# Side work in two places of each block, gates one at a time, and PE in order of emission

## The chip, the core and the metric

The kernel runs on one core of a Trainium2 chip. Time is device time in microseconds (us) of one execution. The engines are PE (TensorE, matrix products), DVE (VectorE), ACT (ScalarE), POOL (GpSimd) and SP (SyncE, which here issues most of the DMA transfers). Each has its own queue and works through it in order. The program is built once: a scheduler fixes the order of every queue when the program is built, and semaphores make the engines wait for one another when it runs.

## The reference

One block of a diffusion backbone: a modulated RMS norm of 4096 tokens of 1024 features, one input projection whose 3072 columns feed two groups, and one output projection.

```python
pl = (rms_norm(xl, norm_g[l]) * (1.0 + sc_l) + sh_l) @ w_in[l]
hf_c, hb_c = rglru_bidir(pc[..., r0:r1], *rnn_p, zero, zero)            # 256 context tokens
hf_l, hb_l = rglru_bidir(pl[..., r0:r1], *rnn_p, hf_c[:, -1], hb_c[:, 0])
# rglru: r = sigmoid(xc @ wa + ba); i = sigmoid(xc @ wx + bx); a = exp(-8 r softplus(-lam))
#        b = sqrt(1 - a^2) * i * xc; h_t = a_t h_(t-1) + b_t, forward and backward
u = dwconv(p[..., :3 * D_HYENA], hy_conv_w, (1, 1)) + hy_conv_b
x0, x1, v = jnp.split(u, 3, axis=-1)
y_h = long_conv(v * x1, kernel, hy_bias) * x0                           # FFT of length 2 x 4096
y = concat([rms_norm(y_h, gn_h) * silu(z_h), rms_norm(hf + hb, gn_r) * silu(z_r)])
xl = xl + g_l * (y @ w_out)
return rms_norm(xl, final_g)
```

The kernel of the long convolution is itself computed: a small network over positions with sines (`mlp`), a product to 1024 filter columns, a decay.

## The kernel before

**Tiling.** Every product is made of three 16-bit products (high by high, high by low, low by high). A block of the input projection (`inproj`, L501) is one strip of 128 output features for 512 tokens: 8 slices of 128 input features times 3 products, 24 matmuls of 512 columns into one bank of tag `mm`, of which there are three. These are the main matmuls. 512 tokens are a chunk. All other matmuls are side work (`mms`, L170, a lower priority for the scheduler) and use tags `fa` and `fb`, two banks each, or `sm`, one bank.

**Pass A** (`pass_a`, L579) goes through chunks 0 to 7, with 12 blocks each: 4 of the recurrent input `xr` and 8 of `x1` and `v`. The list `OX` says how many of the other blocks come before the `xr` blocks in each chunk. A block is followed by its short convolution on ACT and DVE (`conv`) and by stores. The next chunk is loaded, normed, split and transposed beside it (`xload`, `xsplit`).

**Pass B** (`blocks_b`, L1024) has 24 groups of 4 blocks (`zr`, `x0`, `zh`), over chunks from 7 down to 0 in the order of `seq`. Beside it runs a generator `fft` from which `rate` steps are pulled per block: first the transform of the input (`s1u_gen`, evictions `vo`), then 64 slots (`slot_gen`: loads `vu`, `vki`, `tb`, 24 matmuls of 128 columns, a product, a transpose, 3 matmuls of the inverse, eviction `zo` and a store), then the inverse (`inv_block`). The output phase (`phase_out`) multiplies by the output weights.

**Side work and steps.** A counter `step` rises by one per block. `at(d, f)` (L561) files a piece of side work for `d` steps later; `tick` (L565), called after each block, runs what is filed for the step. So all side work of a block is emitted behind its 24 main matmuls. The scheduler then orders each engine's queue, PE's too, by its own estimate of when operands are ready, and may put main matmuls of later blocks ahead of side work that waits.

- `unit` (L804) is a generator for the recurrent part of two strips of features: a split of the input (`xh`), the gates, tanh and exponentials, square roots, scans. Gates: for each lane `l` and gate `g`, 3 matmuls into `fa` (g = 0) or `fb` (g = 1) and a sigmoid on ACT (L824). Two units (`p` = 0, 1) advance together. All gates of a unit lie in one step, 24 matmuls for the two units. `DA` files the steps of pass A (`units_a`, L855), `DC` those of the context, `DS` and `D0` those of pass B (`units_b`, L1092), which end in a total over features (`yscale`, L1147) and a store.
- `filter_group` (L952) files four rows of the filter. `filter_row` (L967) first runs the second half of an earlier row (`second`, `fb`), then 3 matmuls into `fa`, a product with the decay `dec`, a split `kh` and a sum on POOL.
- `wprep` (L463) makes scaled weights: a sum of squares, a total over partitions by a matmul (`total`, L186, operand `p2b`), a scale, a split, and 24 matmuls of 2 columns against `shl` for the bias. `wpair` (L621) runs all of that for two strips in each of the first four steps of chunk 0; `prep` spreads it over three steps in chunk 7.

Of the kernel before, what the change touches and what calls it, by code (L numbers as in the profile page):

```python
# [25 lines left out]
FFT = 1.75  # L26
INV = 1.65
LAG = 3
DC = (1, 2, 4, 5, 5)
CT = 5  # L30
ML = 1
MK = 1
# [10 lines left out]
FL = (2, 3)  # L43
SIDE = 64
FG = 2
OX = (0, 0, 0, 0, 0, 0, 2, 0)
ET = mybir.EngineType
MS = ()
XS = ((1, 2), (1, 2))
PB = {"mm": 3, "fa": 2, "fb": 2, "sm": 1}  # L50
FD = 4.95
XK = ((6, 9), (1, 6))
NX = 11
D0 = (8, 11, 12, 13, 14, 16, 17, 17)
WO = (9, 13, 16)
SEQ = [(2, "zr"), (2, "x0"), (1, "x0"), (1, "zr"), (0, "x0"), (0, "zh"), (0, "zr"), (2, "zh"), (1, "zh")]
XL = [(6, "zr"), (5, "zr"), (4, "zr"), (3, "zr"), (2, "zr"), (1, "x0"), (0, "x0"), (2, "zh")]
DS = (1, 4, 7, 7, 9, 9, 10)
DA = ((11, 12, 14, 15, 15), (3, 4, 4, 6, 6), (0, 3, 5, 6, 8))
EPS = 1e-6  # L60
MAGIC = 1.5 * 2.0 ** 23
INV2PI = 1.0 / (2.0 * math.pi)
# [100 lines left out]
class K:  # L163
# [32 lines left out]
    def build(self):  # L196
        tc = self.tc
        with ExitStack() as es:
            self.dram = es.enter_context(tc.tile_pool(name="dram", bufs=1, space=DRAM))
            self.cp = es.enter_context(tc.tile_pool(name="cp", bufs=1))  # L200
            self.ps = es.enter_context(tc.tile_pool(name="ps", bufs=1, space=PSUM))
            dr = lambda n, s, d=F32: self.dram.tile(s, d, name=n)
            self.s1D = dr("s1D", [2, D])
            self.gD = dr("gD", [1, D])
            self.XD = [dr(f"XD{i}", [128, 2, 8, 512], F16) for i in range(6)]
            self.uD = [dr(f"uD{b}", [128, T]) for b in range(NB)]
            self.VuD = dr("VuD", [128, NB, 64, 256], F16)
            self.VkD = dr("VkD", [128, 64, 1024], F16)
            self.ZD = dr("ZD", [128, 64, 1024], F16)
            self.hD = dr("hD", [128, 2, 64, 64], F16)  # L210
            self.xcD = [dr(f"xcD{b}", [128, T]) for b in range(NB)]
            self.hfD = [dr(f"hfD{b}", [128, T]) for b in range(NB)]
            self.x0D = [dr(f"x0D{b}", [128, T]) for b in range(NB)]
            self.zD = [dr(f"zD0{b}", [128, T]) for b in range(NB)]
            self.hlD = dr("hlD", [128, 8, 2, NB, 512], F16)
            self.consts()
            self.wp = es.enter_context(tc.tile_pool(name="wp", bufs=1))
            self.xp_ = es.enter_context(tc.tile_pool(name="xq", bufs=1))
            self.late = es.enter_context(ExitStack())
            self.todo = {}  # L220
            self.step = 0
            if MS:
                es.enter_context(tc.manual_schedule(engines=set(MS)))
            self.pass_a()
            self.pass_b()
            self.phase_out()
# [271 lines left out]
            w[5] = self.tap_scales(pool, name, j, es[:, 0:1], be[:, 0:1])  # L498
        yield w

    def inproj(self, w, xs):  # L501
        ps = self.pst("mm", 3)
        c = 0
        for x in xs:
            n = x.shape[-1]
            i = 0
            for k in range(8):
                for (wi, xi) in ((0, 0), (0, 1), (1, 0)):
                    self.mm(ps[:, c:c + n], w[0][:, wi, k, :], x[:, xi, k, :], i == 0, i == 23)
                    i += 1  # L510
            c += n
        return ps
# [48 lines left out]
    def at(self, d, f):  # L561

        self.todo.setdefault(self.step + d, []).append(f)

    def tick(self):  # L565
        for f in self.todo.pop(self.step, []):
            f()
        self.step += 1
# [10 lines left out]
    def pass_a(self):  # L579
        tc, nc, a = self.tc, self.nc, self.a  # L580
        with ExitStack() as es, ExitStack() as right:
# [3 lines left out]
            W = {}  # L585
            self.wn = -1
            X = self.xtile()
# [70 lines left out]
            halo = {nm: None for nm in names}  # L658
            nb = [(n, j) for n in ("x0", "zr", "zh") for j in range(NB)]
            self.WB, self.X = {}, {}  # L660
            for i in range(8):
                xcs = []
                for k, nm in enumerate(names[4:4 + OX[i]] + names[:4] + names[4 + OX[i]:]):
                    if i < 7 and k in XK[i > 0]:
# [5 lines left out]
                        if h and i < 5:  # L670
                            self.at(XS[i > 0][1] + 1, lambda i=i, X=Xn: nc.sync.dma_start(self.XD[i + 1], X))
                    j = nm[1]
                    ps = self.inproj(W[nm], [X])
                    p0 = 512 * i - 1 + (1 if i == 0 else 0)
                    if nm[0] == "xr":
                        if j % 2 == 0:
# [29 lines left out]
                X = Xn  # L706
            while any(s < self.step + 8 for s in self.todo):
                self.tick()
    def ctx_in(self, ap, hy, W):
# [18 lines left out]
        for j in range(NB):  # L728
# [3 lines left out]
            if j % 2 == 0:  # L732
# [5 lines left out]
                   for p in range(2)])  # L738
        for d in DC:
            self.at(d, lambda: next(us))  # L740
# [62 lines left out]

    def unit(self, pool, lanes, n, xc, fin, sig=None):  # L804

        nc = self.nc
        L = len(lanes)
        x2 = xc[:, :2 * n]
# [7 lines left out]
        for l, (d, j) in enumerate(lanes):  # L816
            for g, dst, bias in ((0, R, 68 + 4 * d + j), (1, I, 76 + 4 * d + j)):
                for q0 in range(0, n, 512):
                    m = min(512, n - q0)
                    c = n * (j % 2) + q0  # L820
                    ps = self.pst("fa" if g == 0 else "fb", 2)
                    for k, (gi, xi) in enumerate(((0, 0), (0, 1), (1, 0))):
                        self.mms(ps[:, :m], self.gh[d][:, gi, j, g, :], xh[:, 1026 * xi + c:1026 * xi + c + m], k == 0, k == 2)
                    nc.scalar.activation(dst[:, n * l + q0:n * l + q0 + m], ps[:, :m], AF.Sigmoid,  # L824
                                         bias=self.ccol(bias), scale=self.rg[d])
        if sig:
            sig()
        for l in range(0, L, 2):
# [16 lines left out]
        for l, (d, j) in enumerate(lanes):  # L845
            f = (lambda t: t) if d == 0 else (lambda t: t[:, ::-1])
# [105 lines left out]
    def filter_group(self, pool, g):  # L952

        nc = self.nc
        grp = [4 * g + 4 + k for k in range(4)] if g < 15 else [1, 2, 3, 0]
        hb = self.hb[g % 2]
        n0 = min(grp)
        for h in range(2):
            nc.sync.dma_start(hb[64 * h:64 * h + 64, :, :, 64 * h:64 * h + 64],
                              self.hD[64 * h:64 * h + 64, :, n0:n0 + 4, :])  # L960
        dec = pool.tile([128, 4, 512], F32, name="dec", bufs=1)
        for k, n in enumerate(grp):
            nc.scalar.activation(dec[:, k], self.dl, AF.Exp, scale=self.dcol[:, n:n + 1])
        for k, n in enumerate(grp):
            self.at(1 + k, lambda k=k, n=n: self.filter_row(pool, n, hb[:, :, n - n0, :], dec[:, k]))

    def filter_row(self, pool, n, hb, dec):  # L967
        nc = self.nc
        if len(self.sec) > 1:
            self.sec.pop(0)()  # L970
        ps = self.pst("fa", 2)
        for x, (hi, wi) in enumerate(((0, 0), (0, 1), (1, 0))):
            self.mms(ps, hb[:, hi, :], self.whl[:, wi, :], x == 0, x == 2)
# [50 lines left out]
    def blocks_b(self, hy, rn):  # L1024
        tc, nc = self.tc, self.nc
        fft = self.fft_gen()
        gate = self.gate_gen()
        W = self.WB
# [3 lines left out]
        st, X = {}, self.X  # L1032
        done, rate = 0.0, FFT
        for q, (i, nm) in enumerate(seq):
            if (i, nm) in XL:
                k = need.pop(0)
# [12 lines left out]
                    self.at(d, lambda g=st[i]: next(g))  # L1049
            for j in range(NB):  # L1050
                w = W[nm, j]
                ps = self.inproj(w, [X[i]])
                if nm == "zr":
                    if j % 2 == 0:
                        z = rn.tile([128, 1024], F32, name="zr", bufs=2)
# [10 lines left out]
                    if i in (5, 4):  # L1066
                        self.pull(gate, 1)
                self.tick()
                done += rate
                while done >= 1:  # L1070
                    done -= 1
                    self.pull(fft, 1)
                if (i, nm, j) == (0, "x0", 3):
                    self.pull(fft)
                    fft = self.inv_gen()
                    done, rate = 0.0, INV
# [15 lines left out]
    def units_b(self, rn, i):  # L1092
# [14 lines left out]
        def sig(p):  # L1107
            def f():
# [4 lines left out]
        us = zip(*[self.unit(rn, [(1, 2 * p), (1, 2 * p + 1)], 512, xcs[p],  # L1113
                             lambda h, p=p: self.padd(hfs[p], hfs[p], h[:, :1024]), sig(p) if i else None)
                   for p in range(2)])
        for _ in range(4):
            next(us)
            yield
        next(us)
# [431 lines left out]
```

## Time and profile before

| | |
|---|---|
| time, median of 3 runs | 2286.21 us (2283.73 to 2293.96) |
| profiled execution, own time | 2286.44 us |
| its span, first to last instruction | 2284.6 us |
| mean granted clock of PE | 0.927 of full speed |
| busy: PE, DVE, ACT, POOL | 1920.0, 1498.6, 1151.6, 862.5 us |
| matmuls | 10858 |

An engine's idle time is put down to what ended it: "PE fa <- ACT R" is PE waiting to write a bank of tag `fa` or for an operand, until ACT's instruction that writes `R` was done. PE's busy time is the union of its matmuls' lengths, so that matmuls at the lower clock count longer.

### The profile page before, as it was taken

The page shows a single profiled execution, that of the slowest core. Times are in us where ns is not written, and L with a number is a line of the kernel's source. Part 1 is how long each engine was busy: PE and PEld are TensorE (multiplying, and loading weights), DVE is VectorE, ACT ScalarE, POOL GpSimd, SP SyncE. Part 2 cuts the span into 40 slices and gives each one's busy share as a digit, 9 for nine tenths or more (in the row PEclk, how much of TensorE's full clock was granted, in tenths as well). Part 3 has the DMA queues.
Part 4 walks back from the last instruction along what each step waited for, and adds up shares of the span by engine and source line. Part 5 has one row for each costly group of instructions (what it writes and reads, how often), then busy time and mean ns, then how long its engine had stood idle before and what let it go on. Part 6 is the DMA issues. An engine that isn't in the chain of part 4 may idle for free. (4 is left out here: it accounts for less than half of the span.)

```text
span 2284.6 us, 30912 instructions
## 1 busy us (share of the span) xinstructions
PE 1920.0 (84%) x10858; PEld 919.7 (40%) x10858; DVE 1498.6 (66%) x2871; ACT 1151.6 (50%) x1803; POOL 862.5 (38%) x571
## 2 busy tenths in 40 slices
PE   6967769989797889878888999797897766999987
PEld 2434324334343334433334555454544433444433
DVE  4895876857576677664644664755756645777776
ACT  3655766665646577575563633645444412422222
POOL 3024655554656453131322443534433321333330
PEclk9988979989898999999899999998998887999999
DMA  9546244435453322566646999899997799454531
GB/s 291 172 115 168 77 137 137 154 81 162 138 150 96 112 87 96 179 196 207 208 143 210 205 217 249 200 227 244 221 257 206 189 270 230 136 163 155 168 120 74
DMA packets 397608, 391.13 MB, mean 171 GB/s; under 512 B 209513, under 2 KB 295935, under 8 KB 392846
## 3 DMA queue, kind: packets, MB, share of 16 engines
q1 hardware_dynamic: 376988, 342.25, 54.2%
q10 hardware_dynamic: 20466, 46.93, 7.2%
q8 instruction: 85, 1.39, 0.3%
q14 instruction: 69, 0.57, 0.1%
HBM read 213.96 MB, written 132.13 MB: 151 GB/s over the span
## 5 line engine op out<-in xcount | busy, mean ns | idle before, releaser
L168 PE MATMUL mm<-X,wh 128*128 128x512 f16 x3072 | 745.8, 389 | 35.4 <-DMA X<-xh 7.5
L168 PEld LDWEIGHTS <-wh 128*128 128x128 f16 x3648 | 326.5, 100 | 466.9 <-issue 102.3
L168 PE MATMUL mm<-X,wz 128*128 128x512 f16 x1536 | 384.8, 395 | 7.5 <-ACT zh L1064 4.5
L168 PEld LDWEIGHTS <-wz 128*128 128x128 f16 x1728 | 159.9, 101 | 226.7 <-issue 58.0
L168 PEld LDWEIGHTS <-hl 128*128 128x128 f16 x1536 | 151.8, 101 | 212.2 <-issue 20.8
L168 PE MATMUL mm<-wz,hl 128*128 128x512 f16 x768 | 181.8, 395 | 18.9 <-DVE hl L1465 13.4
L168 PE MATMUL mm<-X,hl 128*128 128x512 f16 x768 | 179.9, 389 | 7.7 <-DVE wh L1479 5.3
L985 POOL TENSOR_TENSOR kh<-kd,kh 128x512 f16<-128x512 f32 x64 | 84.5, 1321 | 157.4 <-ACT kh L984 157.4
L460 POOL TENSOR_TENSOR I<-I,xc 128x1024 f32<-128x1024 f32 (+3 forms) x36 | 84.1, 2340 | 128.8 <-ACT I L824 114.8
L1241 POOL TENSOR_TENSOR A<-A,B 128x256 f32<-128x256 f32 x64 | 51.0, 797 | 205.9 <-DVE B L1240 187.8
L452 POOL TENSOR_TENSOR xlo<-xt,xh 128x1024 f16<-128x1024 f32 x32 | 76.8, 2414 | 135.8 <-ACT xh L450 135.8
L168 PE MATMUL fb<-tb,vki 128*128 128x128 f16 x768 | 98.1, 225 | 20.6 <-DMA tb<-in_t_s 19.7
L168 PE MATMUL fa<-xh,gh 128*128 128x512 f16 (+3 forms) x228 | 67.4, 396 | 52.2 <-ACT R L824 42.8
L460 POOL TENSOR_TENSOR zr<-zr,sg 128x1024 f32<-128x1024 f32 x16 | 39.1, 2443 | 176.1 <-ACT sg L1110 176.1
L460 POOL TENSOR_TENSOR xh<-R 128x1024 f32<-128x1024 f32 (+2 forms) x34 | 69.4, 2044 | 79.2 <-ACT R L835 77.7
L1252 DVE SCALAR_TENSOR_TENSOR yy<-A,yy 128x512 f16<-128x512 f32 x64 | 57.7, 902 | 62.1 <-ACT yy L1251 62.0
L841 DVE SCALAR_TENSOR_TENSOR xc<-xh,xc 128x1024 f32<-128x1024 f32 (+2 forms) x34 | 58.2, 1714 | 60.7 <-POOL xh L460 60.3
L168 PE MATMUL fa<-tb,vu 128*128 128x128 f16 x768 | 97.0, 225 | 0.0
L457 POOL TENSOR_TENSOR acc<-acc,dec 128x512 f32<-128x512 f32 x64 | 93.7, 1464 | 4.9 <-ACT dec L978 4.9
L849 DVE TENSOR_TENSOR_SCAN I<-R,car,I 128x512 f32<-128x512 f32 (+2 forms) x64 | 94.6, 1502 | 0.1
L168 PEld LDWEIGHTS <-gh 128*128 128x128 f16 x456 | 46.7, 105 | 111.6 <-issue 70.5
L168 PEld LDWEIGHTS <-vki 128*128 128x128 f16 x768 | 76.7, 100 | 33.7 <-issue 24.5
(377 smaller groups left out, 3723.4 us busy)
## 6 DMA issues: line engine op xcount, KB each, us to landing
VkD<-vk SPq DMA_DIRECT2D x64, 256.0 KB, 2.0
VuD<-vo SPq DMA_DIRECT2D x64, 256.0 KB, 2.5
X<-XD SPq DMA_DIRECT2D x8, 2048.0 KB
vu<-VuD SPq DMA_DIRECT2D x128, 128.0 KB, 3.3
vki<-VkD SPq DMA_DIRECT2D x128, 128.0 KB, 3.6
ZD<-zo SPq DMA_DIRECT2D x64, 256.0 KB, 4.3
xt<-in_x SPq DMA_DIRECT2D x30, 512.0 KB, 5.1
XD<-X SPq DMA_DIRECT2D x6, 2048.0 KB
```

Source lines behind the costliest of these rows:

```text
L168: self.nc.tensor.matmul(out, lhsT, rhs, start=start, stop=stop)
L452: nc.gpsimd.tensor_sub(xl, xt, xh)
L457: self.nc.gpsimd.tensor_add(out, x, y)
L460: self.nc.gpsimd.tensor_mul(out, x, y)
L841: nc.vector.scalar_tensor_tensor(Z, M, 1.0, Z, op0=OP.add, op1=OP.mult)
L849: nc.vector.tensor_tensor_scan(f(h), f(r), f(h), 0.0 if c is None else c, op0=OP.mult, op1=OP.add)
L985: nc.gpsimd.tensor_sub(kh[:, 1], kd, kh[:, 0])
L1241: nc.gpsimd.tensor_sub(A[:, :, 0, :], A[:, :, 0, :], B[:, :, 1, :])
L1252: nc.vector.scalar_tensor_tensor(yy[:, :, 1, :], yv, 0.125, yy[:, :, 0, :], op0=OP.mult, op1=OP.subtract)
```

## The change

- `inproj` takes a function `mid`, called between the fourth and the fifth of its 8 slices. What is filed for a half step is run there, so side work has two places per block: between the halves of the 24 main matmuls and behind them. In pass B half of `rate` is pulled from `fft` at each of the two places.
- `unit` yields after each gate, so that the gates of one lane and kind (6 matmuls for the two units) are a step of their own. `DC`, `DA`, `DS` and `D0` get more entries, with half steps.
- The second half of a filter row is filed for the half step ahead of the next row.
- In chunk 1, four `x1` and `v` blocks come before the `xr` blocks.
- From the first chunk on, to the end of the program, PE takes its instructions in the order of emission. The other engines' queues are still ordered by the scheduler.

```diff
-DC = (1, 2, 4, 5, 5)
+DC = (1, 2, 2, 2.5, 2.5, 3, 3, 3.5, 3.5, 4, 5, 5)
...
-OX = (0, 0, 0, 0, 0, 0, 2, 0)
+OX = (0, 4, 0, 0, 0, 0, 2, 0)
...
-D0 = (8, 11, 12, 13, 14, 16, 17, 17)
+D0 = (8, 11, 11.5, 12, 12.5, 13, 13, 14, 16, 17, 17)
...
-DS = (1, 4, 7, 7, 9, 9, 10)
-DA = ((11, 12, 14, 15, 15), (3, 4, 4, 6, 6), (0, 3, 5, 6, 8))
+DS = (1, 3, 3.5, 4.5, 5.5, 7, 7, 9, 9, 10)
+DA = ((11, 12, 12.5, 13, 13.5, 14, 15, 15), (1, 2, 2.5, 3, 3.5, 4, 5, 6), (0, 2, 2.5, 3.5, 4.5, 6, 7, 9))
...
+                if mid and k == 4:
+                    mid()
                 for (wi, xi) in ((0, 0), (0, 1), (1, 0)):
                     self.mm(ps[:, c:c + n], w[0][:, wi, k, :], x[:, xi, k, :], i == 0, i == 23)
...
+    def mid(self):
+        for f in self.todo.pop(self.step - 0.5, []):
+            f()
+
     def tick(self):
+        self.mid()
         for f in self.todo.pop(self.step, []):
             f()
         self.step += 1
...
+            self.es.enter_context(tc.manual_schedule(engines={ET.PE}))
             for i in range(8):
...
-                    ps = self.inproj(W[nm], [X])
+                    ps = self.inproj(W[nm], [X], self.mid)
...
+                if (l, g) != (L - 1, 1):
+                    yield
         if sig:
             sig()
...
         for k, n in enumerate(grp):
+            self.at(0.5 + k, lambda: len(self.sec) > 1 and self.sec.pop(0)())
             self.at(1 + k, lambda k=k, n=n: self.filter_row(pool, n, hb[:, :, n - n0, :], dec[:, k]))
...
-        if len(self.sec) > 1:
-            self.sec.pop(0)()
...
+                def mid():
+                    nonlocal done
+                    self.mid()
+                    done += rate / 2
+                    while done >= 1:
+                        done -= 1
+                        self.pull(fft, 1)
+                ps = self.inproj(w, [X[i]], mid)
...
-                done += rate
+                done += rate / 2
...
-        for _ in range(4):
+        for _ in range(7):
             next(us)
             yield
```

## Rows read from the trace of the kernel before

**Rows 1.** The profile's page: span, and busy time by engine (share of span, instructions).
```profile
span 2284.6 us, 30912 instructions
...
PE 1920.0 (84%) x10858; PEld 919.7 (40%) x10858; DVE 1498.6 (66%) x2871; ACT 1151.6 (50%) x1803; POOL 862.5 (38%) x571
```
**Rows 2.** Stretches: length; busy PE, PEld, DVE, ACT, POOL (count); clock, DMA share, GB/s.
```profile
61.00:206.00 145.00, 110.03 (x853) 60.39 (x851) 121.03 (x363) 83.18 (x143) 32.17 (x20) 0.89 0.52 145
206.00:917.00 711.00, 604.83 (x2803) 264.24 (x2804) 494.09 (x865) 459.07 (x771) 376.18 (x235) 0.92 0.41 121
...
206.00:335.00 129.00, 93.33 (x395) 39.46 (x396) 92.72 (x149) 89.96 (x143) 71.10 (x41) 0.87 0.34 102
335.00:421.00 86.00, 79.05 (x357) 35.13 (x357) 55.84 (x98) 56.41 (x94) 48.31 (x32) 0.98 0.48 140
...
1258.00:1700.00 442.00, 389.91 (x2873) 220.96 (x2873) 276.98 (x438) 213.41 (x345) 178.46 (x162) 0.97 0.95 226
```
**Rows 3.** PE timeline (start, length of the run); then PE's groups in 206 to 917.
```profile
336.67 12.54 PE L168 MATMUL mm<-X,wh 128*128 128x512 f16 x54
...
L168 PE MATMUL sm<-shl,wh 128*128 128x2 f16 x168 | 6.2, 164 | 1.0 <-ACT wh L478 0.7 <-DVE wh L483 0.2
```
**Rows 4.** What PE waited for in 206 to 917: us in total, times, longest.
```profile
PE fa L168 <- ACT R L824: 32.7, 6, 14.5
PE fb L168 <- DVE car L851: 14.0, 1, 14.0
...
PE fb L168 <- DVE vk L996: 11.0, 2, 10.4
```
**Rows 5.** The same for 61 to 206, 917 to 1258 and 1258 to 1700.
```profile
PE fa L168 <- ACT R L824: 7.2, 2, 6.3
...
PE fa L168 <- DVE vo L1201: 32.3, 13, 8.9
...
PE fb L168 <- DMA tb<-in_t_s: 19.7, 13, 3.4
PE fb L168 <- DVE zo L1266: 7.6, 5, 5.2
```
**Rows 6.** Timelines of POOL, ACT and PE around 690: start, length, [idle before <- releaser].
```profile
682.62 1.26 POOL L457 TENSOR_TENSOR xt<-xt,rp 128x512 f32<-128x512 f32 x1 [5.08 <-issue]
...
687.46 2.56 ACT L963 ACTIVATE dec<-dl,dcol 128x512 f32<-128x512 f32 x4 [8.54 <-POOL acc L457]
...
694.90 1.44 PE L168 MATMUL fa<-xh,gh 128*128 128x512 f16 x3 [14.47 <-ACT R L824]
```
**Rows 7.** PE timeline of one weight pair in chunk 0.
```profile
76.91 0.17 PE L168 MATMUL sm<-p2b_w,onesb 128*128 128x1 bf16 x1
...
78.52 0.20 PE L168 MATMUL sm<-shl,wh 128*128 128x2 f16 x2
78.59 1.45 PE L168 MATMUL mm<-X,wh 128*128 128x512 f16 x6
79.88 0.69 PE L168 MATMUL sm<-shl,wh 128*128 128x2 f16 x22
80.44 1.24 PE L168 MATMUL mm<-X,wh 128*128 128x512 f16 x5
81.51 0.74 PE L168 MATMUL sm<-shl,wh 128*128 128x2 f16 x24
```
**Rows 8.** Groups by line over the whole span: busy us, mean ns | idle before.
```profile
L824 ACT ACTIVATE R<-fa,col,p2r_g 128x512 f32<-128x512 f32 (+2 forms) x76 | 54.9, 732 | 7.7 <-PE fa L168 7.0
...
L975 DVE TENSOR_TENSOR kd<-fa,dec 128x512 f32<-128x512 f32 x64 | 43.6, 682 | 24.8 <-PE fa L168 17.7 <-POOL kh L985 5.2 <-ACT dec L963 1.8
...
L824 ACT ACT_TABLE_LOAD x10 | 12.8, 1283 | 1.8 <-DVE I L849 1.6
```
**Rows 9.** What PE waited for in 1700 to 1950, and in 1950 to the end.
```profile
PE sm L168 <- DVE p2b_yr L189: 10.6, 2, 8.3
...
PE mm L168 <- DVE hl L1465: 13.4, 5, 4.3
```

More of the change, by code (lines that the diff above doesn't have):

```diff
@@ L45 @@
 FG = 2
-OX = (0, 0, 0, 0, 0, 0, 2, 0)
+OX = (0, 4, 0, 0, 0, 0, 2, 0)
 ET = mybir.EngineType
-MS = ()
 XS = ((1, 2), (1, 2))
@@ L221, in build @@
             self.step = 0
-            if MS:
-                es.enter_context(tc.manual_schedule(engines=set(MS)))
+            self.es = es
             self.pass_a()
@@ L499, in wprep, with inproj @@
         yield w
-    def inproj(self, w, xs):
+    def inproj(self, w, xs, mid=None):
         ps = self.pst("mm", 3)
@@ L1051, in blocks_b @@
                 w = W[nm, j]
-                ps = self.inproj(w, [X[i]])
+                def mid():
[6 more added lines that the diff above has]
+                ps = self.inproj(w, [X[i]], mid)
                 if nm == "zr":
```

## The prediction, made before the changed kernel was run

> **What bounds the kernel now.** I read the page first. TensorE (PE) is busy for 1920.0 of 2284.6 us [rows 1] and no other engine comes near, so the question is what its 365 us of idle time and its slow stretches are made of. I then cut the span at the first main matmul of each stage and asked for busy time by stage [rows 2]. 24 main matmuls make a block and 288 a chunk of pass A. The stages are chunk 0 (61 to 206), chunks 1 to 7 (206 to 917), and of pass B the input transform (to 1258), the 64 slots (to 1700) and the inverse (to 1950); then comes the output phase.
>
> A run of 54 matmuls of 512 columns takes 12.54 us, the last one's 0.38 of length included, so one costs 0.216 us at full clock [rows 3]. Chunks 1 to 7 hold 2803 matmuls [rows 2], of which 168 are two columns wide and take 6.2 us together [rows 3] and some 45 are small; the other 2590 need 2590 x 0.216 = 559 us. With the small ones that is 566 us of work. PE was busy for 604.8 of the 711 us [rows 2]. So 106 us are idle and 39 us are work at the lower of the two clocks (1.2 against 2.4 GHz), which stands behind the idle stretches: chunk 2 (335 to 421), with little idle, was granted 0.98 and took 86 us, while the stage as a whole was granted 0.92 [rows 2]. Seven chunks at 86 us are 602: this stage could give at most 109 us.
>
> The waits of that stage name the loss [rows 4]. 32.7 us in 6 waits are PE waiting for a sigmoid (ACT R L824), 14.0 us is one wait in the same gate work, and 11.0 us (10.4 of them in one wait) is a filter matmul of chunk 1. These are few and long: 57.7 us in 9 waits, 6.4 us on average. The longest shows the mechanism [rows 6]. POOL waits 5.08 us ahead of an addition to x; ACT's exponentials wait 8.54 us for POOL; the sigmoids stand behind them on ACT; both banks of tag fa are full; PE stands for 14.47 us at the fifth gate of a clump of eight, with the main matmuls queued behind it. Elsewhere the same pattern is smaller: 7.2 us in chunk 0, 32.3 us in 13 waits for the eviction `vo` of the input transform [rows 5]. In the slots the longest item is a load (`tb`, 19.7 us [rows 5]) and the DMA engines are busy for 0.95 of the stage [rows 2], so little is to be had there.
>
> **Part by part.** No matmul is added or removed; only places and orders change.
>
> *Gates one at a time.* The 24 gate matmuls of a chunk's two units were emitted in one step; now there are four places half a block or more apart, each with one gate of both units (6 matmuls, two banks). Half a block is 12 x 0.216 = 2.6 us of cover, against two sigmoids of 0.73 us [rows 8]. A stall of ACT of 8 us is then met by one or two blocks of main work, not by none. Of the 57.7 us I take two thirds as gained, 38 us. Of the 39 us of slow clock the same waits own 57.7/106 = 54%, 21 us, two thirds of it 14 us. The sum is 52; half of the 109 us of the chunk view is 55. I take 50, since POOL's wait for the load of x stays, and 0 and 109 as the ends.
>
> *New meetings in a bank.* The gates now share three of their four places in a chunk with a filter row (fa) or its second half (fb). Those are three users of a tag with two banks, and the third waits for an eviction of 0.7 us (L824, L975 [rows 8]) plus that engine's queue, less the 0.65 us of the second user's three matmuls. I take 0.8 us x 3 places x 7 chunks = 17 us (0 to 40).
>
> *Half-step pulls in pass B.* One pull at a time instead of one or two at the end of a block: half of the 32.3 us, 16, and 4 us of slow clock in proportion to pass A (16 x 14/57.7); in the slots most of the 7.6 us behind `zo` [rows 5], 5 us. Sum 25 (0 to 45).
>
> *Context gates in chunk 0.* 7.2 us [rows 5] go: 7.
>
> *PE in order of emission.* This is what costs. PE may no longer pull main matmuls of the next block into a gap. In chunk 0 each of four pairs of weights emits its two totals and its 48 bias matmuls in one step. In the trace the second total is at 76.91 and ends at 77.08; the bias matmuls can start at 78.52, 79.88 and 81.51, as their weights are scaled and split, and main matmuls fill the gaps [rows 7]. In order, PE stands for 81.51 - 77.08 = 4.4 us less the 0.89 us of bias work between, 3.5 us, four times, 14 us, and with some queue on VectorE 17 us (0 if VectorE, busy 121 of 145 us there [rows 2], sets the pace anyway; 28 at twice the 3.5). The main blocks and the filter network's matmuls are queued behind it.
>
> In pass B the gates now end at step 5.5 and not at 4, while the total of `yscale` stays at step 9; what stands between (tanh, exponentials, square roots, scans, additions) has 3.5 blocks instead of 5. Two waits there already cost 10.6 us, the longest 8.3 [rows 9]. For the 8 chunks I take 1 us each, 8 (0 to 8 x 8.3 = 66). In the output phase each of seven chunks has a total in the middle of its main matmuls; waits for `hl` are 13.4 us now [rows 9] and I take no change (13 gained to 7 x 4.3 = 30 lost). The filter's setup, its final sum and the weight preparation of chunk 7 each have a chain that PE used to step over: together 8 us (0 to 25), an estimate from the 3.5 us above, some twice.
>
> *The queues.* The new places also move what the steps issue: the second half's store to SP moves half a block earlier than the row that follows; `units_a`'s stores move one step later; in chunk 1 the recurrent blocks move behind four convolution blocks, with their stores. All stay within buffers that are two deep. I cost these at nothing; the cover is the 0.41 DMA share of pass A [rows 2], and without it a store that blocks an eviction costs a few us a chunk.
>
> *Sum.* 50 - 17 + 25 + 7 - 17 - 8 - 8 = 32 us by the middle values. Chunk 1 (206 to 335) is 43 us longer than chunk 2 [rows 2], and it is the one whose order is changed (context steps, recurrent blocks in the middle). Its two long waits, 14.0 and 10.4 us, are in the 50 with two thirds, 16; of the other 27 us I take two thirds too, 18. That makes 50 us from the profiled run of 2286.4 us (span 2284.6 and 1.8 around it; the median of the runs shown is 2286.2), so **2236 us**.
>
> **The rivals.** *The waits go altogether.* All seven chunks run like chunk 2 (109), the transform's 32.3 us and the context's 7.2 go, less the 17 of chunk 0: 2286 - 131 = 2155 us. For it: chunk 2 does it now. Against: its units fall where ACT is free, and the loads of x that POOL waits for stay.
>
> *The waits only move.* PE meets a stalled ACT one block later and stands there for the same time, as the root is POOL's wait for a load [rows 6], which no edit touches. Then half of the 50 comes and none of the 18: 2286 - 25 - 25 - 7 + 50 = 2279 us. Against: three accumulators of tag mm let main work run on for a block or two.
>
> *The lost cover decides (slower).* Place: the totals. If `yscale` costs 8.3 us per chunk (66), chunk 0's pairs 28, the output phase 30 and the small chains 8, that is 132 us against 82 gained by gates, pulls and context, so 2336 us. It decides as soon as the new waits pass 82 us. For it: nothing in the old trace shows PE held to emission. Against: all other engines may still run ahead, so that most operands can be there before PE comes to them.
>
> *Table loads.* Sigmoids in four places can each need their own table: now 10 loads at 1.283 us [rows 8] serve 17 pairs of units (8 chunks in each pass and the context); at four each there would be 68, 58 more, 74 us of ACT time, and as many on the way back for exponentials. If only the first 74 us land on PE's path the time is 2236 + 74 = 2310 us. Against: ACT is busy for 459 of 711 us in pass A [rows 2], so most lands in idle time.
> The Trainium skill (ScalarE: Activation LUTs, Table sets: the hidden batching unit) says that activations should be batched by table set, which speaks against splitting the gates. It gives some 2.7 us for a switch; the row has 1.283 us for the load itself, and the measured one is used. By its figure this rival would be at 2236 + 58 x 2.7 = 2393 us.
>
> **How the numbers follow.** The forecast, 2236 us, has 0.58 with its own range of 2175 to 2273; the waits gone 0.14; moved 0.10; lost cover 0.12; table loads 0.06. 0.5% of the time is 11 us, about what a measurement of this kernel can tell from no change. Faster by more than that is 0.58 + 0.14 = 0.72, within it 0.10, slower 0.18. The range for 8 in 10 leaves half of the first rival out below and most of lost cover above: 2160 to 2310.
>
> **What would show it.** Right: in the new trace waits of PE for ACT R L824 in pass A fall to a third, none over 6 us, and chunks come to 88 to 95 us with the clock at 0.95 or more; `vo` waits halve; `p2b_w`, absent in chunk 0 now, shows there with 3 to 5 us four times. Wrong: PE waits for `p2b_yr` over 25 us in sum (lost cover), over 40 table loads at L824 with ACT waits behind them (tables), or the same long waits at another tile (moved). The sum would be most wrong if the 18 us of chunk 1 don't come, or if DMA, at 0.95 in the slots, is met worse by a PE that can't step aside.

## The result and the profile after

The changed kernel takes 2432.3 us (median of 4 runs, 2429.2 to 2438.1) beside 2285.0 for the kernel before on the same chip: a ratio of 1.0646, 95% interval 1.0613 to 1.0679. It is 147 us slower; the forecast was 50 faster. The profiled run took 2429.2 us.

The page's span and busy times answer to [rows 1]:
```profile
span 2426.1 us, 30971 instructions
...
PE 1944.6 (80%) x10858; PEld 939.4 (39%) x10858; DVE 1513.2 (62%) x2871; ACT 1174.6 (48%) x1813; POOL 846.4 (35%) x571
```
The work is the same, 10858 matmuls. PE's idle time grew from 365 to 481 us; its busy time grew by 25, which is the same matmuls at the lower clock. So the change cost waits, and the stretches by stage say where (columns as in [rows 2]: chunk 0, chunk 1, chunk 7, the slots):
```profile
61.00:235.00 174.00, 114.64 (x818) 58.62 (x817) 115.38 (x363) 77.67 (x129) 25.76 (x16) 0.77 0.44 123
235.00:375.00 140.00, 103.39 (x429) 45.07 (x429) 82.51 (x137) 93.78 (x150) 68.29 (x44) 0.84 0.36 113
875.00:1030.00 155.00, 103.08 (x686) 48.41 (x685) 98.30 (x228) 83.87 (x133) 29.75 (x19) 0.81 0.31 103
1365.00:1827.00 462.00, 382.14 (x2789) 220.74 (x2788) 266.79 (x432) 215.13 (x340) 178.57 (x162) 0.91 0.89 213
```
By the same cut (first main matmul of each stage) chunk 0 took 145 us before and takes 174; chunk 7 took 95 and takes 155; chunks 1 to 6 took 615 and take 640. The row of chunk 7 before, for comparison:
```profile
822.00:917.00 95.00, 89.35 (x575) 41.00 (x573) 74.90 (x164) 70.50 (x119) 37.85 (x22) 0.98 0.29 95
```
What PE waited for, over the whole span (us in total, times, longest):
```profile
PE sm L167 <- DVE p2b_yr L188: 89.6, 7, 17.8
PE fb L167 <- ACT I L831: 42.8, 16, 12.1
PE sm L167 <- DVE p2b_w L188: 26.8, 8, 9.0
PE sm L167 <- DVE p2t_yh L192: 22.1, 8, 3.4
PE mm L167 <- DMA X<-xh: 21.5, 3, 18.1
PE fa L167 <- ACT R L831: 21.1, 14, 8.7
```
Three of these are waits for totals (`p2b_yr`, `p2b_w`, `p2t_yh`), all in the one bank of tag `sm`. Before, `p2b_yr` stood at 15.2 us in the whole span and `p2t_yh` at 1.6. The waits for the sigmoid `R` fell, in chunks 1 to 7 from 32.7 [rows 4] to 17.0; `I`, the second sigmoid of a gate, came up as a new name with 39.2 there.

The longest wait for `p2b_yr`, on PE, then on ACT and on DVE (start, length, [idle before <- releaser]):
```profile
1094.46 2.75 PE L167 MATMUL mm<-X,wz 128*128 128x512 f16 x12
1115.00 0.16 PE L167 MATMUL sm<-p2b_yr,onesb 128*128 128x1 bf16 x1 [17.79 <-DVE p2b_yr L188]
...
1118.01 4.70 PE L167 MATMUL mm<-X,wz 128*128 128x512 f16 x12
```
```profile
1109.55 0.19 ACT L1151 ACTIVATION_READ_ACCUMULATOR sg<-zr 128x1 f32 x1
```
```profile
1107.88 3.41 DVE L817 TENSOR_SCALAR xh<-xc,p2s_xr 128x1024 f16<-128x1024 f32 x2
1111.22 3.48 DVE L818 SCALAR_TENSOR_TENSOR xh<-xc,p2s_xr,xh 128x1024 f16<-128x1024 f32 x2
1114.62 0.14 DVE L1167 TENSOR_REDUCE q1r<-qs 128x1 f32<-128x2 f32 x1
1114.79 0.16 DVE L188 CAST p2b_yr<-q1r 128x1 bf16<-128x1 f32 x1
```
The matmul is one column wide (0.16 us). It is emitted at its step, and PE stands for 17.79 us until VectorE has the number. For 12.5 us of that the chain itself isn't done, on VectorE and ACT; ACT's last sum is there at 1109.74. The last 5.0 us before the cast at 1114.79 are VectorE's queue: it was splitting the next unit's `xh` (6.8 us in all), which came first. Twelve main matmuls, which need nothing from VectorE, come only at 1118.01, and then run 4.70 us instead of 2.75, as PE comes back at the lower clock (granted 0.61 of full speed in 1118 to 1123, 1.00 in 1094 to 1097). The Trainium skill (PSUM — Partial Sum Buffer, Engine vs sequencer instructions) says that matmuls start and complete in program order; these rows agree, so what is emitted ahead of a matmul is its cover or its obstacle.

### The profile page after: what moved, and what is told of

The parts are those of the page before. It is cut to its first block, busy times and chain, and to the rows that moved or that the text cites. A ratio compares the mean times of both kernels' runs of the same rounds, so it can differ in the third digit from the quotient of the medians.

```text
span 2426.1 us, 30971 instructions
## 1 busy us (share of the span) xinstructions
PE 1944.6 (80%) x10858; PEld 939.4 (39%) x10858; DVE 1513.2 (62%) x2871; ACT 1174.6 (48%) x1813; POOL 846.4 (35%) x571
## 5 line engine op out<-in xcount | busy, mean ns | idle before, releaser
L167 PEld LDWEIGHTS <-wh 128*128 128x128 f16 x3648 | 333.7, 101 | 471.1 <-issue 113.4
L167 PE MATMUL mm<-X,wz 128*128 128x512 f16 x1536 | 375.0, 400 | 0.0
L1268 DVE SCALAR_TENSOR_TENSOR yy<-A,yy 128x512 f16<-128x512 f32 x64 | 52.4, 818 | 88.5 <-ACT yy L1267 88.5
L455 POOL TENSOR_TENSOR acc<-acc,dec 128x512 f32<-128x512 f32 x64 | 98.3, 1536 | 15.3 <-ACT dec L986 15.2
L1004 DVE TENSOR_TENSOR vk<-fb,vk 128x512 f16<-128x512 f32 x64 | 43.8, 684 | 90.5 <-ACT vk L1003 87.8
L167 PE MATMUL fb<-kh,st 128*128 128x512 f16 x192 | 56.2, 396 | 48.6 <-ACT I L831 36.6
L1267 ACT ACTIVATE yy<-A 128x512 f16<-128x512 f32 x64 | 40.2, 629 | 109.1 <-POOL A L1258 74.7
L1217 DVE TENSOR_TENSOR vo<-fa,vo 128x512 f16<-128x512 f32 x64 | 43.8, 686 | 73.6 <-ACT vo L1216 73.0
L167 PE MATMUL fa<-xh,gh 128*128 128x512 f16 (+3 forms) x228 | 55.7, 374 | 37.8 <-DVE kd L983 17.8
L1255 DVE TENSOR_TENSOR A<-fa,kf 128x512 f32<-128x512 f32 x64 | 44.0, 687 | 63.3 <-ACT kf L1251 50.4
```

What stands on the lines that cost most here:

```text
L167: self.nc.tensor.matmul(out, lhsT, rhs, start=start, stop=stop)
L455: self.nc.gpsimd.tensor_add(out, x, y)
L1004: nc.vector.tensor_sub(vo[:, :, 1, :], pv, vo[:, :, 0, :])
L1217: nc.vector.tensor_sub(vo[:, :, 1, :], pv, vo[:, :, 0, :])
L1255: nc.vector.tensor_mul(A, u4, kf[:, :, 0:1, :].to_broadcast([128, NB, 2, 64]))
L1267: nc.scalar.activation(yy[:, :, 0, :], yv, AF.Copy, scale=0.125)
```

## The experiments

All were timed against the kernel before on the same chip (median 2284 to 2285 us). Stage lengths below are cut as above.

**Order alone, split alone.** To the kernel before, the first adds only the line that holds PE to the order of emission; the second is the changed kernel without that line.
```
+            self.es.enter_context(tc.manual_schedule(engines={ET.PE}))
             for i in range(8):
```


> The kernel before with one part of the change alone: PE in order of emission from the first chunk on. Gates stay eight at a time, side work stays behind the block. Theory 1 (the order takes away the cover of short chains: a total over partitions, then a scale, then the next matmul): this alone is slower than the kernel before by at least the 147 us of the whole change, 2430 to 2560 us, since the clumps of 24 gate matmuls on two banks per tag are then met in order too; PE waits for p2b_yr and p2b_w together over 60 us (before: 32 us). Theory 2 (the split gates, half steps and table loads cost the time, the order does not): 2270 to 2310 us.

> The changed kernel without the order of emission: gates one at a time, side work in two places, new step lists, but PE ordered by the scheduler as before. Theory 1 (order): 2230 to 2300 us, PE waits for p2b_yr near the 15 us of before, and the 147 us are gone. Theory 2 (splitting): 2380 to 2440 us, with 16 table loads at the sigmoid line as in the changed kernel and ACT waits behind them.


Measured: the order alone 2400.6 (1.0507, 1.0489 to 1.0525), the split alone 2314.8 (1.0134, 1.0119 to 1.0149). So +116 and +30; together 147, what the whole change costs. Both parts lose, and they add up; neither theory's ranges were met (2430 to 2560 and 2270 to 2310 for the first run, 2230 to 2300 and 2380 to 2440 for the second). With the order alone chunk 0 is 30 us longer, chunk 7 73; chunks 1 to 6 sum to 611 us (615 before). The waits for `p2b_yr` over the whole span, with the order alone and with the split alone:
```profile
PE sm L168 <- DVE p2b_yr L189: 6.8, 1, 6.8
```
```profile
PE sm L167 <- DVE p2b_yr L188: 48.6, 6, 12.4
```
So the largest wait of the changed kernel comes from the split's new steps (15.2 us before); with the order added it is 89.6, but the order alone doesn't bring it. With the order alone `p2b_w` leads, with 48.4 us.

**The total later; two raw buffers.** Two cures inside the changed kernel. The first emits the units of pass B earlier and the total a step later; the second loads chunk 7's weights into two buffers, not one.
```
-D0 = (8, 11, 11.5, 12, 12.5, 13, 13, 14, 16, 17, 17)
+D0 = (8, 11, 11.5, 12, 12.5, 13, 13, 14, 16, 18.5, 19)
...
-DS = (1, 3, 3.5, 4.5, 5.5, 7, 7, 9, 9, 10)
+DS = (1, 2, 2.5, 3.5, 4.5, 6, 6, 8, 10, 10.5)
```
```
+    raw = ap.tile([128, D], F32, name="xt", bufs=2)...
+    nc.sync.dma_start(raw, a["w_in"][...])
-    self.prep(self.WB, nb[k])
+    self.prep(self.WB, nb[k], raw=raw)
```


> The changed kernel with other steps in pass B alone: gates one step earlier, the total of yscale at step 10 and not 9, so that the chain between has 5.5 blocks and not 3.5; for the last chunk 18.5 and not 17. Theory 1 (PE in order stands at p2b_yr until the chain is done): the 90 us of waits for p2b_yr fall to under 25 us and the time to 2345 to 2375 us. Theory 1b (the waits only move, because DVE, ACT and DMA set the pace of pass B): p2b_yr falls but the time stays over 2415 us, with other waits in its place.

> The changed kernel with a second buffer for the raw weights that chunk 7 prepares (the two buffers that held tokens, free by then, in place of the one buffer wr). Theory 1 (in chunk 7 PE in order stands once per block for load, sum of squares and total, because the next load waits for the last reader of the one buffer): chunk 7 falls from 155 us to 100 to 115 us and the time to 2375 to 2395 us. Theory 1c (what stands there is the chain behind the total, and DVE): chunk 7 stays over 140 us, the time over 2415 us.


Measured: 2418.7 (1.0586, 1.0568 to 1.0603) and 2423.6 (1.0610, 1.0582 to 1.0638), 14 and 9 us better than the changed kernel, though for the second the two intervals overlap. With the total later the waits for `p2b_yr` in the input transform fall from 47.2 us to nothing, and those for `vo` there rise from 10.1 to 29.0. That is theory 1b. With two buffers chunk 7 goes from 155 to 139 us: short of the 100 to 115 of theory 1, a hair under the 140 of theory 1c, whose time (over 2415) it was. The places are right, but a cured wait is mostly replaced by the next.

**The order place by place.** The kernel before with the order held in some stages alone, and (the first run) the changed kernel with it in chunks 1 to 6 alone.
```
+                self.ordered(0 < i < 7)      # or: i in (0, 7), 2 < i < 7
```
```
+            self.ordered(q < 9)              # transform; or from q == 9 to the end
```


> The changed kernel with PE held to the order of emission in chunks 1 to 6 of pass A alone. Theory P (place): the order costs only where a short chain from PE over another engine back to PE is emitted in one piece (chunk 0's weight pairs, chunk 7's weights, the totals of pass B); those places are free again here, so the time is that of the split alone, 2315, within 10 us either way. Rival S (split and order add up where the split put the gates): chunks 1 to 6 sum to 640 us in the changed kernel and to 619 with the split alone, so 21 us stay: 2336.

> The kernel before (gates in one step) with PE held to the order of emission in chunks 1 to 6 and in the input transform of pass B, free elsewhere. With the order everywhere these stages were 5 us and 26 us shorter than in the kernel before. Theory P (place): these are gains of their own, as PE no longer takes main matmuls ahead of what the other engines wait for: 2284 - 31 = 2253. Rival G (given back): the 26 us are only what chunk 7's stall had let the other engines do ahead, so without the stall they don't come: 2284 - 5 = 2279.

> The kernel before with PE held to the order of emission in chunks 0 and 7 alone. With the order everywhere chunk 0 was 30 us longer and chunk 7 73 us. Theory P (place): both come and nothing is given back: 2284 + 103 = 2387. Rival G (given back): the input transform is 26 us shorter behind a stalled chunk 7: 2361. If the order in the stages between fed the stalls: under 2340.

> The kernel before with PE held to the order of emission from the tenth main group of pass B (the slots, the inverse, the output phase) to the end. With the order everywhere the slots were 11 us longer, the inverse 40 us longer and the output phase 18 us shorter. Theory P (place): the same again, 2284 + 33 = 2317. Rival (late start): the inverse was longer only because what ran before it had been late; then under 2300.


Measured: 2325.7 (1.0186, 1.0166 to 1.0206); 2293.4 (1.0037, 1.0022 to 1.0052); 2359.3 (1.0331, 1.0312 to 1.0350); 2326.0 (1.0189, 1.0165 to 1.0212). The three places cost 8, 74 and 41 us, 123 in all against 116 in one kernel. So the order costs by place, and three fifths of it in chunks 0 and 7. The 8 us of the second run are two things: chunks 1 to 6 are 8 us shorter there (607), the transform is 21 longer (362 for 341). Neither theory had the transform right: there is no gain of 26 us. Its stage had looked shorter in part because the order leaves main matmuls for later: with the order alone 912 main matmuls fall into it, before 960 (48 x 0.216 = 10 us), and the inverse has 503 instead of 360. What the other 16 us were stays open. A stage table must be read with its matmul counts. The 2359 of the third run is rival G's number, but not for its reason: the transform is 339 us long there, as before, and chunk 7 is 56 us longer, not 73. With the split, chunks 1 to 6 cost 11 us more in order, between the two expectations.

Chunk 0 (60 to 238) and chunk 7 (850 to 1002) with the order there alone, and the largest waits of each:
```profile
60.00:238.00 178.00, 123.73 (x855) 63.43 (x855) 121.42 (x368) 84.64 (x146) 30.18 (x20) 0.79 0.42 119
850.00:1002.00 152.00, 109.00 (x630) 49.18 (x629) 99.14 (x209) 83.83 (x135) 36.23 (x22) 0.84 0.29 98
```
```profile
PE sm L168 <- DVE p2b_g L189: 12.8, 2, 8.9
PE sm L168 <- DVE be L495: 6.1, 7, 2.0
```
```profile
PE sm L168 <- DVE p2b_w L189: 26.4, 8, 4.4
PE sm L168 <- DVE xc L525: 10.2, 1, 10.2
```
Chunk 0 ran 853 matmuls in 110.0 us at a granted clock of 0.89 [rows 2]; here 855 take 123.7 at 0.79. So of its 33 us some 19 are idle time and 14 the clock. The clock is a second price that the waits bring.

In the slots with the order from there on (1266 to 1728), the stretch and the waits that rose:
```profile
1266.00:1728.00 462.00, 385.45 (x2780) 224.51 (x2781) 257.19 (x431) 212.25 (x337) 171.86 (x162) 0.91 0.87 213
```
```profile
PE fb L168 <- DMA tb<-in_t_s: 28.1, 12, 5.2
PE fb L168 <- ACT kf L1245: 26.2, 13, 4.7
PE sm L168 <- DMA wr<-in_w_mod: 11.2, 2, 7.2
```
Before, these were 19.7, 0.7 and 4.1 us. DMA's share falls from 0.95 [rows 2] to 0.87: that a PE which stands for one load holds up the stores that make room for the next would do this, but it was not isolated. The slots run 889 main matmuls instead of 984 (95 x 0.216 = 21 us of work) and take 15 us longer, a loss of 36 us of the 41. The other stages sum to the rest: the transform ahead is 3 us longer with 48 main matmuls fewer, the inverse 40 longer with 143 more, the output phase 18 shorter with some 165 matmuls fewer.

**Which part of the split costs.** From the split alone, the gates of pass B put back into one step; then the half-step pulls taken out too; then the pulls alone on the kernel before.
```
-D0 = (8, 11, 11.5, 12, 12.5, 13, 13, 14, 16, 17, 17)
+D0 = (8, 11, 12, 12, 12, 12, 13, 14, 16, 17, 17)
...
-DS = (1, 3, 3.5, 4.5, 5.5, 7, 7, 9, 9, 10)
+DS = (1, 4, 4, 4, 4, 7, 7, 9, 9, 10)
```
```
-                ps = self.inproj(w, [X[i]], mid)
+                ps = self.inproj(w, [X[i]], self.mid)
...
-                done += rate / 2
+                done += rate
```


> The split alone (PE free), but the units of pass B emit their gates in one step again; the pass A side work and the half-step pulls of pass B stay as changed. The split alone took 2315, and of its 30 us over the kernel before 21 lie in pass B. Theory G (the split gates of pass B cost them): 2294. Rival H (the half-step pulls cost them): 2315 still.

> As the kernel of the run before it, with whole-step pulls in pass B again, so that only the side work of pass A is split. Theory G: 2294, as with half-step pulls. Rival H: 2294 here and 2315 there. The forecast's own step (half-step pulls gain 25): 25 slower than with them. A third way: what pass A leaves behind makes pass B longer, then 2315 in both.

> The kernel before with nothing but the half-step pulls of pass B. The forecast's step: 25 faster, 2260. Nothing gained, since the evictions that the waits are for run behind the same work of ACT and VectorE: 2285, within 6. Rival H (they cost): 2300 or more.


Measured: 2300.7 (1.0075, 1.0044 to 1.0106); 2290.1 (1.0021, 1.0000 to 1.0042); 2293.3 (1.0038, 1.0019 to 1.0057). So the split gates of pass B cost 14 us, the half-step pulls 11 here and 9 alone, the side work of pass A 6 (its interval begins at 1.0000). Both theories hold in part. Waits in the input transform, first the split alone, then with pass B's gates in one step, then the pulls alone:
```profile
PE sm L167 <- DVE p2b_yr L188: 21.4, 3, 9.8
```
```profile
PE sm L167 <- DVE p2b_yr L188: 6.0, 1, 6.0
```
```profile
PE fa L168 <- DVE vo L1210: 30.0, 14, 8.4
```
The 15 us between the first two, with PE free, fit the price of gates that end at step 5.5 with the total still at 9; moving the total alone was not tried with PE free. The last, 30.0 against 32.3 before [rows 5], is what half-step pulls did for `vo`: nothing.

**Order where it looked good.** Chunks 3 to 6 alone.


> The kernel before with PE held to the order of emission in chunks 3 to 6 alone. With the order in chunks 1 to 6 and the transform these four took 388 us and not 400. If that is a gain of its own: 2273. If it is given back behind them, as the 26 us of the transform were: 2285, within 6.


Measured: 2275.8 (0.9963, 0.9945 to 0.9980): 8 us faster than the kernel before, the one version that beats both, though by less than half a per cent. Chunks 3 to 6 sum to 390 us (400 before). It is a gain of its own, but too small to build on: with the split added it is gone (below).

**Links apart.** The order in chunks 0 and 7 again (2359), but each chain's links emitted apart, and the same without the order as a control. Chunk 0's pairs advance one link per block, the context's gate weights too (and `recur`, which frees the weights' buffers, moves from step 3 to 5); chunk 7's advance one link in two blocks, with two raw buffers.
```
-                for _ in range(3):
-                    for h in range(2):
-                        W[names[k + h]] = next(gs[h])
+                def link(): ...
+                link(); self.at(1, link); self.at(2, link)
...
-                        self.prep(self.WB, nb[k])
+                        self.prep(self.WB, nb[k], 2, raw=raw)
```


> Order of emission in chunks 0 and 7 alone, as in the run that took 2359, but with the links of the short chains emitted apart: each pair of chunk 0 a tick between load and square, total, and bias matmuls; the context's gate weights a tick between square and total; chunk 7's weights two ticks, with two raw buffers. Theory C (the order costs where a chain from PE over another engine back to PE is emitted without main work between its links): of the 74 us at least half goes, so 2322 or less. Rival R (PE in order simply follows the slower engines, wherever the links stand): only the 9 us that two raw buffers gave before, 2350.

> The same links apart, PE free as in the kernel before: the control. Theory C: with PE free the cover comes from the planner anyway, so 2285 within 6. If it is faster or slower, the difference between this run and the one before it is what the order still costs.


Measured: 2319.5 (1.0162, 1.0133 to 1.0190) and 2303.6 (1.0090, 1.0066 to 1.0115). The first is under the 2322 of theory C, if barely: of the 74 us 36 are left. The control is itself 20 us slower than the kernel before, 14 of them in the transform behind, so this is no cure; and the 16 us between the two flatter the order, since the transform is 17 us shorter with it (337 for 354). In the two chunks it still costs 29 us over the control, where it had cost 88: chunk 0 takes 169 us for 151, chunk 7 112 for 100. So the theory holds in chunk 7, which goes from 152 to 112 us, and its timeline shows why:
```profile
844.00:956.00 112.00, 94.45 (x579) 44.46 (x578) 86.88 (x198) 77.13 (x131) 35.64 (x22) 0.92 0.32 103
```
```profile
893.69 0.16 PE L168 MATMUL sm<-p2b_w,onesb 128*128 128x1 bf16 x1
893.72 5.34 PE L168 MATMUL mm<-X,wh 128*128 128x512 f16 x24
```
This total comes with no wait ahead of it, and `p2b_w` (26.4 us with the links in one piece) is no longer among the chunk's waits. Compare the changed kernel (SP's queue, ACT, DVE, PE):
```profile
901.48 0.33 SPq L467 DMA_DIRECT2D wr<-in_w_in  x1
```
```profile
905.13 1.06 ACT L471 ACTIVATE wh<-wr 128x1024 f16<-128x1024 f32 x1 [0.72 <-DMA wr<-in_w_in]
...
906.31 0.16 DVE L188 CAST p2b_w<-wq 128x1 bf16<-128x1 f32 x1 [2.23 <-ACT wh L471]
...
906.52 0.16 PE L167 MATMUL sm<-p2b_w,onesb 128*128 128x1 bf16 x1 [4.27 <-DVE p2b_w L188]
```
One raw buffer: its load is issued at 901.48, when VectorE has just split the block before (to 901.45), lands 3.6 us later, is squared and cast, and PE stands for 4.27 of the 5.0 us from the issue to its matmul. In chunk 0 spreading did little (178 to 169 us). `p2b_g` is still 12.5 us:
```profile
PE sm L168 <- DVE p2b_g L189: 12.5, 1, 12.5
```
```profile
156.56 0.19 ACT L794 ACTIVATION_READ_ACCUMULATOR gh<-wr 128x1 f32 x1
...
162.49 0.14 DVE L189 CAST p2b_g<-gq 128x1 bf16<-128x1 f32 x1
```
ACT has the sum at 156.75; VectorE casts it 5.7 us later, behind the filter network's and the convolution's work. For these 5.7 of the 12.5 us the cover that PE lacks is room in VectorE's queue.

**Where the gates' gain went.** The split of pass A alone, with the filter's second half emitted with its row again; and that with the order in chunks 3 to 6.
```
-            self.at(0.5 + k, lambda: len(self.sec) > 1 and self.sec.pop(0)())
...
+        if len(self.sec) > 1:
+            self.sec.pop(0)()
         ps = self.pst("fa", 2)
```


> Only the side work of pass A split (2290), but the filter's second half emitted with its row again and not half a block ahead of it. In that kernel the waits for the sigmoids R fell, while those of the second half for kh came to 23 us, from 6. Theory K (the half step less of cover for kh is what ate the gates' gain): the kh waits fall under 10 and the time to 2275. Rival M (the lost time moves again, as ACT and POOL stand for the loads of x): 2290, with the waits at other tiles.

> The kernel of the run before it with PE in order in chunks 3 to 6. Order in these chunks alone gave 2276. If the two gains add up: 2275 - 8 = 2267. If they are the same time: 2275. With split gates the order had no gain in these chunks (the changed kernel spends 390 us there, the split alone 401, but the rest gave it back), so under rival M: 2285.


Measured: 2280.9 (0.9992, 0.9979 to 1.0004) and 2286.2 (1.0018, 1.0003 to 1.0033). Waits in chunks 1 to 7 with the split of pass A alone (210 to 926), then with the second half back (206 to 910):
```profile
PE fa L167 <- ACT R L830: 15.1, 3, 10.2
PE fb L167 <- POOL kh L992: 13.1, 8, 4.7
PE fb L167 <- ACT I L830: 12.8, 4, 5.1
PE fb L167 <- ACT kh L991: 9.8, 3, 4.6
```
```profile
PE fb L167 <- ACT I L830: 14.8, 5, 4.4
PE fa L167 <- DVE kd L983: 14.2, 5, 5.1
PE mm L167 <- DVE xc L530: 11.6, 6, 5.5
PE mm L167 <- DMA X<-xh: 10.6, 3, 6.8
PE fb L167 <- POOL kh L993: 10.4, 4, 4.5
...
PE fa L167 <- ACT R L830: 5.0, 4, 2.0
```
`R` falls from 32.7 [rows 4] to 15.1 and then to 5.0, and no single wait is over 7 us. Yet the stage goes from 711 to 716 and 704 us. In the last run `I` has 14.8 us, which was no name there before, and `xc` 11.6 for 1.7, `kh` 10.4 for 4.4, `kd` 14.2 for 11.0. Theory K gave 9 of the 15 us between its number and rival M's; `kh` went from 22.9 to 10.4 us while `kd` went from 2.1 to 14.2. So the split of the gates without the moved second half is worth nothing clear of noise (0.9992), where 58 us had been forecast, and the order in chunks 3 to 6 adds nothing to it (2286.2, beside rival M's 2285): the waits come back at other tiles, which is rival M. That loads of x are at its root, as M has it, was not tried.

## Why the prediction was wrong

By parts, in us (plus is slower), each measured as a difference of the runs above:
```
part                                      forecast   measured
side work of pass A split                      -58         +6
half-step pulls in pass B                      -25   +9, +11
split gates of pass B, total where it was       +8        +14
order in chunks 0 and 7                   +17 to 25        +74
order from the slots to the end                  0        +41
order in chunks 1 to 6 and the transform         0         +8
sum                                            -50       +154
the whole change                               -50       +147
```
Two steps failed: the gain booked for waits that go (83 us forecast for pass A's split and the half-step pulls, 15 to 17 lost), and the price of the order (17 to 25 us forecast, 116 measured).

*Gates one at a time* (50, with 18 for chunk 1, 7 for the context, less 17). The mechanism failed, not the size. The first half of the step was right: the waits for `R` fell by half and then to 5 us. The second half, that a wait which disappears is time gained, was not: the rival "the waits only move" is what pass A shows. Chunk 1 did come down, from 129 to 113 us with the split of pass A alone, half of the 34 that the sum took for it (16 for its two long waits and 18 more); chunk 2 went from 86 to 104. I had read chunk 2 as what a chunk costs without waits; but the two together take 215 us before and 217 then, which fits a chunk 2 that was short because chunk 1 had been long. This was not tested apart. In the changed kernel one long wait stands ahead of chunk 1's first main matmul, inside the 174 us of chunk 0:
```profile
234.79 0.59 PE L167 MATMUL mm<-X,wh 128*128 128x512 f16 x1 [18.12 <-DMA X<-xh]
```
The transposes that fill this `X` are issued from 227.83 us on, behind ACT's split of x, which starts at 226.75. The wait is there too, with 15.3 us, when the split kernel is held to the order in chunks 1 to 6 alone; what makes ACT late was not tried.

Two figures of the working were off. The 0.216 us doesn't follow from the run of 54 in 12.54 us, which gives 0.229; it is what other runs give (24 in 5.34 us above, by the same working), so the sums made with it stand. And the rest of chunk 1 is 43 less 24.4, 19 us and not 27, so 12 and not 18, and the forecast 2242.

*Half-step pulls* (25). The waits for `vo` didn't halve (30.0 against 32.3), so the gain taken from them never came, and the kernel with nothing but these pulls became 9 us slower; where those 9 us lie was not isolated.

*New meetings in a bank* (17) were about the right size, but came at the filter's second half: waits of tag fb for `kh` rose from 4.4 to 22.9 us, by 18.5, with the split of pass A alone; putting the second half back gave 9 us of time.

*Order of emission, chunk 0* (17). The pairs cost what was worked out: in the run with the order there alone `be` 6.1 and `wh` and `wz`, from ACT and from VectorE, 11.2, together 17.3 us. The sign named for it, `p2b_w` with 3 to 5 us four times, was the wrong name: in the changed kernel it has 1.3 us in chunk 0. What was missing are the context's gate weights (`p2b_g` 12.8, for 2.2 before) and the clock, 14 us. The gains of the sum carried a term for the clock; its losses had none.

*The small chains* (8, 0 to 25). This is the mis-sized term: the order makes chunk 7 alone 56 us longer, and spreading the links of its weights over two raw buffers takes 40 of them away. The estimate was "3.5 us, some twice"; but there are twelve blocks of weights, and PE waits for `p2b_w` eight times; and the chain through the one raw buffer is longer than a block: even in the kernel before its loads are issued 8 to 11 us apart, while 24 main matmuls take 5.3. The count was in the code, and the price was taken from chunk 0, where the weights lie in buffers loaded ahead.

*`yscale`* (8, 0 to 66). The wait has the place named, and with split and order it is 89.6 us instead of 15.2, 74 more and above my upper end; in time it is less, since moving the total took 47.2 of these us away and gave 14 back. The 1 us a chunk had no row behind it. In the wait shown above the chain itself makes 12.5 of the 17.8 us, and VectorE's queue ahead of the cast 5.0.

*Output phase and slots* (0). In the output phase that held by the waits: `p2t_yh` 22.1 us came, while `hl` fell from 13.4 [rows 9] to 2.6 and a wait for `p2b_yh` of 9.2 went. In the slots I took the DMA share of 0.95 for a reason that little changes; the forecast named a PE that can't step aside there among its dangers, but its sum had nothing for it, and the order cost 36 us.

*Table loads* were not it by the sign named for them (over 40): at the sigmoids' line 16 for 10, in the whole span 77 for 67, each the same length.
```profile
L831 ACT ACT_TABLE_LOAD x16 | 20.5, 1283 | 0.3
```
Ten more at 1.283 us are 13 us of ACT. The Trainium skill's rule (ScalarE: Activation LUTs, Table sets: the hidden batching unit), weighed in the forecast, holds in direction, but by these rows it decides nothing here.

The rival "the lost cover decides" was the right one in its mechanism and its direction. Its sign (`p2b_yr` over 25 us) came, but tells the order's loss from the split's poorly, since the split alone has 48.6 us of it and the order alone 6.8. That its upper ends add up to 132 us, near the 116 to 123 of PE in order, is luck: half of them was `yscale`, 30 the output phase, which lost nothing, and 8 the small chains, while the runs put 74 us in chunks 0 and 7 and 41 from the slots on, where the mechanism stays open. The 82 us set against it on the other side never came. The chance of 0.12 was too small because "all other engines may still run ahead" was taken for cover: they do, but each in its own queue, and the one number that PE stands for may still be being made, or be last in it.

## What to carry to other kernels

Before an engine is held to the order of emission, list every small instruction on it that needs a number from another engine (totals, transposes, bias sums, one-bank tags) and price each by its chain on the other engines and the longest queue ahead of it there, times its count; then emit its links with main work between, or leave that stage free. A wait that vanishes is a gain only if the engine that was late has room later: look for what is late next before booking it. Price the lost clock with every new wait, and compare stages by their matmul counts as well as their length.

## What the runs showed of the hardware that was not expected

Idle time on PE cost about 1.7 times itself in chunk 0 with the order there: 19 us more of idle time, in waits of at most 8.9 us, went with 14 us more for nearly the same matmuls, at a granted clock of 0.79 instead of 0.89 (of two levels, 1.2 and 2.4 GHz). In chunk 7 of that run it was 1.5 times: 37 us more idle (43.0 for 5.7) in a stage 56 us longer, at 0.84 instead of 0.98, with 55 matmuls more. And a stage in which the DMA engines were busy for 0.95 of the time still lost 36 us when PE alone was held to an order, with their share going to 0.87.
